# A one-core hybrid attention layer: first modulation sums shared with TensorE, an accumulator per token tile at the end, another machine model in the scheduler

## The chip, the cores and the metric

One core of a Trainium2 chip runs the whole layer in one launch. The metric is the device time in microseconds (us) of one execution; the median over several executions is quoted, and one further execution is recorded by the hardware profiler.

## What is computed

One decoder layer on 256 tokens of 2048 channels, in float32:

```
mod = silu(c) @ w_ada + b_ada                      # 2048 -> 3 x 2048: shift, scale, gate
h = rms_norm(x, g_pre) * (1 + scale) + shift
proj = h @ w_in                                    # 2048 -> 20032
a  = mla(q, kv_a) * silu(z_mla);    y_mla = a @ w_mla_proj      # 16 heads, causal, low-rank k and v
bb = dilated(qkv) * silu(z_dil);    y_dil = bb @ w_dil_proj     # 3 groups x 8 heads, softmax over all 3
merged = sigmoid(gl_mla) * y_mla + sigmoid(gl_dil) * y_dil
out = merged @ w_o
x = x + gate * rms_norm(out, g_post)
```

## The kernel before, in words

**Projections.** Tokens stand in two tiles t of 128. Every weight block goes through `load_split` (L227): a DMA on SP's queue brings 512 KB as `raw` (8 buffers), ScalarE (ACT) rounds it to the high part `whi` (L235), VectorE (DVE) subtracts to get the low part `wlo` (L236; 4 buffers each). `multiply` (L239) then makes three products on TensorE (PE), hi x hi, hi x lo and lo x hi, as matmuls of 128 tokens by 512 columns (L246). One projection group of 512 output columns is 8 such blocks, 96 matmuls, into one accumulator `acc`. In most of the kernel there are two accumulators; a group is copied out by ACT (L578 and others) before its accumulator serves the next group but one.

**Start.** `w_ada` is needed before the first h. Its shift and scale columns come in 7 pieces (`PIECES`, 3 blocks of 128 channels in the first). For a piece, DVE multiplies each of 16 row blocks with a column of silu(c) and adds it to `ada` (L172, L174); matmuls with ones (`pt_ada`, L187) add over the partitions; `adasc`, `colmul` and `colsh` are made from that (L189 to L192) and `make_h` (L203) builds the operand hTh, hTl. While piece 1 is summed, PE has nothing to do but `keep_busy` matmuls whose result is not used (L150). Later pieces are summed while PE works through the groups listed in `head` (`visit`, L526).

**Attention between projections.** `dil_attention(quad)` (L468) does four heads, twice. A head D: transposes of q and k and their copies (`qk_t`, L452), then for each t three score matmuls (s_D, L482), the masked maximum on DVE (L435), the exponential on ACT (L439), transposes of the probabilities (pt_pD, L448), a copy by ACT (L449), the product with v (pv_D, L491) and DVE's product with the gate (L493). After the quad, `transpose_split` (L417) turns the result for the projection. The MLA loop (L626) has f = 0 to 3, each with two pairs j of two heads M: scores s_M (L667 to L671), exponentials (L683), pt_pM, pv_M (L689 to L691), the gate product `av` (L694), and after four heads `transpose_split` to aT (L698); each f begins with the gate group `zm` whose SiLU (L629) empties its accumulator. In both, every step waits for the one before it.

**End.** `acc_o` groups of 512 or 256 columns; ACT squares each (L746), DVE multiplies it with the gate (L747). The last 256 columns are computed for t = 0, then t = 1, in one accumulator `acc_last` (L755); then the norm, and four adds of 512 columns with a DMA each (L766, L768).

**Order.** The program text gives dependencies. In which order an engine executes its instructions is chosen by the tile scheduler when the context at L789 closes, from its own model of how long everything takes. Each engine then runs its list strictly in that order.

Of the kernel before, what the change touches and what calls it, by code (L numbers as in the profile page):

```python
# [9 lines left out]
F32 = mybir.dt.float32  # L10
# [3 lines left out]
ALU = mybir.AluOpType  # L14

P = 128
S = 256
D = 2048
KC = D // P
# [17 lines left out]
W_BUFS = 4  # L37
H_BUFS = 3
QK_BUFS = 4
WARM = 6  # L40
U_BUFS = 27
SCRATCH = 1024
PIECES = (3, 2, 3, 2, 2, 2, 2)
# [30 lines left out]
def hybrid_block(ctx: ExitStack, tc: tile.TileContext, x, c, positions, w_ada, b_ada, g_pre, g_post,  # L74
                 w_in, g_kv, w_kv_b, w_mla_proj, w_dil_proj, w_o, table, out):
    nc = tc.nc
    V, A, T = nc.vector, nc.scalar, nc.tensor

    cp = ctx.enter_context(tc.tile_pool(name="cp", bufs=1))
# [5 lines left out]
    def slot(shape, name, dt=F32):  # L85
        return up.tile(shape, dt, tag="u", name=name)

    def acc_tile(name):
        return banks["pool"].tile([P, 2, 512], F32, tag="acc", bufs=banks["acc"], name=name)

    def tp_tile(shape, name):
        return banks["pool"].tile(shape, F32, tag="b", bufs=banks["b"], name=name)
# [5 lines left out]
    xr = x[0].rearrange("(t p) d -> p t d", p=P)  # L98
    crow = cp.tile([16, P], F32, tag="crow", name="crow")
    rows = cp.tile([52, P], F32, tag="rows", name="rows")  # L100
# [4 lines left out]
    ident = tid[:, 0:P]  # L105
# [3 lines left out]
    for q in range(4):  # L109
        t = slot([P, 2, 512], f"xn{q}")  # L110
# [6 lines left out]
    ones = cp.tile([P, P], F32, tag="ones", name="ones")  # L117
# [3 lines left out]
    ccol = cp.tile([P, 16], F32, tag="ccol", name="ccol")  # L121
    pt = tp_tile([P, 16], "pt_c")
# [24 lines left out]
    def keep_busy(v):  # L147

        idle = tp_tile([P, 512], "idle")
        T.matmul(idle[:, :v.shape[-1]], ident, v, start=True, stop=True)  # L150

    def ada_steps(pi):

        a, nk = starts[pi], PIECES[pi]
        n = nk * P
        kb = max(1, RAW // (2 * n))
        acc = slot([P, 2, n], f"ada{pi}")
        steps = []
        src = w_ada[0].rearrange("(k p) (j d) -> p k j d", p=P, d=D)
        flat = acc.rearrange("p j n -> p (j n)")  # L160
        pt = tp_tile([P, 2, nk], f"pt_ada{pi}")

        def one(k0, kn):
            raw = wp.tile([P, RAW], F32, tag="raw", bufs=RAW_BUFS, name=f"raw_a{pi}_{k0}")
            v = raw[:, :kn * 2 * n].rearrange("p (k j n) -> p k j n", j=2, n=n)
            for k in range(kn):
                nc.sync.dma_start(v[:, k], src[:, k0 + k, 0:2, a * P:a * P + n])
            for k in range(kn):
                kk = k0 + k
                w = raw[:, k * 2 * n:(k + 1) * 2 * n]  # L170
                if kk == 0:
                    V.tensor_scalar(flat, w, ccol[:, kk:kk + 1], None, op0=ALU.mult)  # L172
                else:
                    V.scalar_tensor_tensor(flat, w, ccol[:, kk:kk + 1], flat, op0=ALU.mult, op1=ALU.add)  # L174
                if pi == 0 and kk >= KC - WARM:
                    keep_busy(v[:, k, 0, :])

        for k0 in range(0, KC, kb):
            steps.append(lambda k0=k0: one(k0, min(kb, KC - k0)))

        def finish():
            sc = sp.tile([P, 4], F32, tag="adasc", name=f"adasc{pi}")
            parts = [(b, b + 1) for b in range(nk)] if pi == 0 else [(0, nk)]
            for lo, hi in parts:
                for b in range(lo, hi):
                    for j in range(2):
                        T.matmul(pt[:, j, b:b + 1], acc[:, j, b * P:(b + 1) * P], ones[:, 0:1],  # L187
                                 start=True, stop=True)
                V.tensor_add(sc[:, lo:hi], pt[:, 1, lo:hi], bsc[:, a + lo:a + hi])  # L189
                V.scalar_tensor_tensor(colmul[:, a + lo:a + hi], sc[:, lo:hi], 1.0, gpre[:, a + lo:a + hi],  # L190
                                       op0=ALU.add, op1=ALU.mult)
                V.tensor_add(colsh[:, a + lo:a + hi], pt[:, 0, lo:hi], bsh[:, a + lo:a + hi])  # L192
                make_h(a + lo, a + hi)
            if pi == 0:
                for _ in range(2):
                    keep_busy(acc[:, 0, :])

        return steps, finish

# [63 lines left out]

    win = w_in[0]


    ssx = cp.tile([P, 2, 4], F32, tag="ssx", name="ssx")
    xT = []
    for q in range(4):
        xT.append(slot([P, 4, S], f"xT{q}"))  # L270
        for hp in range(2):
            pt = tp_tile([P, 2, 2, P], f"pt_x{q}{hp}")
# [5 lines left out]
        for t in range(2):  # L278
            j = sp.tile([P, 768], F32, tag="sm", name=f"junk_x{q}{t}")
            if t == 0:  # L280
                A.activation(j[:, 0:512], xn[q][:, t, :], AF.Square, accum_out=ssx[:, t, q:q + 1])
            else:
                V.tensor_tensor_reduce(j[:, 0:512], xn[q][:, t, :], xn[q][:, t, :], 1.0, 0.0,
                                       op0=ALU.mult, op1=ALU.add, accum_out=ssx[:, t, q:q + 1])
# [9 lines left out]
    pt = tp_tile([P, S], "pt_r")  # L294
    T.matmul(pt, ones, rdiag.rearrange("p t n -> p (t n)"), start=True, stop=True)
    V.tensor_copy(rstdT, pt)

    cols = cp.tile([P, 52], F32, tag="cols", name="cols")
    pt = tp_tile([P, 52], "pt_cols")
    T.transpose(pt, rows, ident[0:52, 0:52])  # L300
    V.tensor_copy(cols, pt)
    bsh, bsc, gpre = cols[:, 0:16], cols[:, 16:32], cols[:, 32:48]
    gkv = cols[:, 48:52]


    gacc = [None, None]
    gg = [None, None]
# [235 lines left out]
    for pi in range(len(PIECES)):  # L543
# [4 lines left out]
        if last:  # L548
            head_ps.__exit__(None, None, None)
            banks.update(pool=ctx.enter_context(tc.tile_pool(name="ps", bufs=1, space=bass.MemoryType.PSUM)),  # L550
                         acc=2, b=4)
# [21 lines left out]
    for g in range(1, 3):  # L573
        for s in range(3):
            nm = f"d{s}{g}1"
            acc = group(hT, win, KC, dil_col(s, g, 1), 512, nm)
# [7 lines left out]
    for t in range(2):  # L584
        j = sp.tile([P, 768], F32, tag="sm", name=f"junk_kv{t}")
# [7 lines left out]
    for k in range(4):  # L593
        pt = tp_tile([P, 2, P], f"pt_ckv{k}")
# [8 lines left out]
    for t in range(2):  # L603
        v = kpe[:, t:t + 1, :]
        rope(kp[:, t:t + 1, 0:64], v, cosM[:, t, 0:1, :], sinM[:, t, 0:1, :], 64, f"kp{t}")
    V.tensor_copy(kp[:, :, 64:128], kp[:, :, 0:64])
    pt = tp_tile([P, 2, P], "pt_kp")
# [9 lines left out]
    for h in range(2):  # L617
        r, o = slice(h * 64, (h + 1) * 64), slice((1 - h) * 64, (2 - h) * 64)
# [7 lines left out]
    for f in range(4):  # L626
        acc = group(hT, win, KC, C_ZMLA + f * 512, 512, f"zm{f}")
# [3 lines left out]
        for pr in range(2):  # L631
            j = 2 * f + pr
            gate_some(KC // UK // 2)
            while mq_done < 384 * (j + 1):
                acc = group(hT, win, KC, mq_done, 512, f"mq{mq_done // 512}")
# [7 lines left out]
            acc = group(ckv, wkv, 4, j * 512, 512, f"kv{j}")  # L643
# [5 lines left out]
            pt = tp_tile([P, 2, P], f"pt_qp{j}")  # L649
# [5 lines left out]
            for h in range(2):  # L655
                r, o = slice(h * 64, (h + 1) * 64), slice((1 - h) * 64, (2 - h) * 64)
                A.copy(qst[r, h, :], flat[r])
                V.tensor_tensor(qst[o, h, :], flat[r], qst[r, h, :].bitcast(F32), ALU.subtract)
            for h in range(2):
# [4 lines left out]
                for t in (1, 0):  # L664
                    nk = (t + 1) * P
                    o = 0 if t else S
                    T.matmul(sc[:, o:o + nk], qk[:, 0, t * P:(t + 1) * P], qk[:, 1, 0:nk],  # L667
                             start=True, stop=False)
# [5 lines left out]
                for t in (1, 0):  # L674
                    nk = (t + 1) * P
                    o = 0 if t else S
                    V.tensor_tensor_reduce(sm[:, o:o + nk], sc[:, o:o + nk], mm[t], 1.0, -3e38,
                                           op0=ALU.add, op1=ALU.max, accum_out=st[:, t:t + 1])
                V.tensor_scalar(st[:, 2:4], st[:, 0:2], -SC_MLA, None, op0=ALU.mult)
                for t in (1, 0):  # L680
                    nk = (t + 1) * P
                    o = 0 if t else S
# [10 lines left out]
                for t in range(2):  # L693
                    V.scalar_tensor_tensor(av[:, t, hs], pv[:, t, :], st[:, 6 + t:7 + t], zm[:, t, hs],  # L694
                                           op0=ALU.mult, op1=ALU.mult)
# [7 lines left out]
    part = []  # L703
    for n in range(4):
        acc = group(hT, win, KC, C_GLD + n * 512, 512, f"gd{n}")
        sg = slot([P, 2, 512], f"sgd{n}")
        A.activation(sg, acc, AF.Sigmoid)
        acc = group(bbT, w_dil_proj[0], 8, n * 512, 512, f"yd{n}")
# [3 lines left out]
    for n in range(4):  # L712
        acc = group(hT, win, KC, C_GLM + n * 512, 512, f"gm{n}")
# [16 lines left out]


    ssq_o = cp.tile([P, 2, 5], F32, tag="sso", name="sso")
    xre = []
    for n in range(4):
        t = slot([P, 2, 512], f"xre{n}")
        nc.scalar.dma_start(t, xr[:, :, n * 512:(n + 1) * 512])
        xre.append(t)
    ov = [slot([P, 2, 512], f"ov{n}") for n in range(4)]
    outr = out[0].rearrange("(t p) d -> p t d", p=P)
    blocks = [(0, 512), (512, 512), (1024, 512), (1536, 256), (1792, 256)]  # L740

    def out_block(i, t, acc):
        c0, n = blocks[i]
        m, o = divmod(c0, 512)
        j = sp.tile([P, 768], F32, tag="sm", name=f"junk_o{i}{t}")
        A.activation(j[:, 0:n], acc[:, t, :n], AF.Square, accum_out=ssq_o[:, t, i:i + 1])  # L746
        V.tensor_mul(ov[m][:, t, o:o + n], acc[:, t, :n], gg[m // 2][:, m % 2, o:o + n])  # L747

    for i, (c0, n) in enumerate(blocks[:-1]):
        acc = acc_tile(f"acc_o{i}")  # L750
        run(acc, mT, w_o[0], 0, KC, c0, n, f"o{i}")
        for t in range(2):
            out_block(i, t, acc)
    c0, n = blocks[-1]
    acc = acc_tile("acc_last")  # L755
    tiles = [(k, kn) + load_split(w_o[0], k, kn, c0, n, f"last_{k}") for k, kn in chunks(0, KC, n)]
    for t in range(2):
        for k, kn, whi, wlo in tiles:
            multiply(acc, mT, whi, wlo, k, kn, n, k == 0, k + kn == KC, (t,))
        out_block(4, t, acc)  # L760
        sq = cp.tile([P, 1], F32, tag=f"sq{t}", name=f"sq{t}")
        V.reduce_sum(sq, ssq_o[:, t, :], axis=mybir.AxisListType.X)
        ro = cp.tile([P, 1], F32, tag=f"ro{t}", name=f"ro{t}")
        rsqrt_mean(ro, sq, D, f"ro{t}", 1)
        for m in range(4):
            V.scalar_tensor_tensor(xre[m][:, t, :], ov[m][:, t, :], ro, xre[m][:, t, :],  # L766
                                   op0=ALU.mult, op1=ALU.add)
            (nc.sync if m % 2 else nc.scalar).dma_start(outr[:, t, m * 512:(m + 1) * 512], xre[m][:, t, :])  # L768


_INS = ("x", "c", "positions", "w_ada", "b_ada", "g_pre", "g_post", "w_in", "g_kv", "w_kv_b",
# [21 lines left out]
```

## Time and profile before

| | us |
|---|---|
| median of 3 runs | 1297.11 (1294.25 to 1297.4) |
| the profiled execution, its own time | 1296.44 |
| its span in the trace | 1294.6 |

Around the span lie 1296.44 - 1294.6 = 1.8 us. The page gives each engine's busy time over the span, then 40 slices; PEclk is TensorE's granted clock in tenths of full speed. The chain of waits follows the last instruction back to what released it; the wait view adds up, by instruction and releaser, the time in which an engine had nothing to run.

### The profile page before, as it was taken

Reading aid. Unit: us, or ns where it says so; the run is one execution under the profiler, and the core shown is the slowest. Engines: PE = TensorE matmul, PEld = TensorE weight load, DVE = VectorE, ACT = ScalarE, POOL = GpSimd, SP = SyncE. Lnnn points to the kernel's source line nnn. Section 1 sums busy time; section 2 is a strip of 40 time slices with the busy share of each in tenths; the row PEclk is TensorE's granted clock in tenths of the full one; section 3 lists DMA queues with packets and bytes.
Section 4 is the critical chain, followed back from the end, with each engine's and each line's share of the span. In section 5 each row is a group of like instructions: output and inputs, shape, how many; then the busy total and the mean of one; then the engine's idle time right before and its main releaser. Section 6 shows DMA issues by size and latency. Waiting matters only on the chain.

```text
span 1294.6 us, 16408 instructions
## 1 busy us (share of the span) xinstructions
PE 1263.7 (98%) x6063; PEld 1046.1 (81%) x6063; DVE 828.1 (64%) x1210; ACT 600.4 (46%) x775; POOL 0.2 (0%) x4
## 2 busy tenths in 40 slices
PE   4999999999999999999999999999999999999996
PEld 3888888888888888888878888788888888888886
DVE  6878887996974445549666585675444444565545
ACT  2555334344365444455545555555444444434442
POOL 0000000000000000000000000000000000000000
PEclk8899999999999999999999999999999999999999
DMA  9899988986552566526667485674666665565741
GB/s 331 297 309 328 319 276 283 309 281 215 170 158 82 182 194 195 164 79 206 233 205 256 125 318 159 209 250 127 193 194 193 195 195 195 198 221 184 259 147 65
DMA packets 158971, 275.00 MB, mean 212 GB/s; under 512 B 9574, under 2 KB 46636, under 8 KB 158892
## 3 DMA queue, kind: packets, MB, share of 16 engines
q1 hardware_dynamic: 156564, 268.70, 64.1%
q10 hardware_dynamic: 2328, 5.27, 1.2%
q8 instruction: 47, 0.77, 0.2%
q14 instruction: 32, 0.26, 0.1%
HBM read 271.83 MB, written 2.10 MB: 212 GB/s over the span
## 4 chain that ended last, share of the span: by engine, by line
PE 95%; DVE 3%; DMA 1%; ACT 1%; issue 1%; SPq 0%; DVEq 0%; ACTq 0%
PE acc_d L246 30%; PE acc_mq L246 10%; PE acc_gd L246 7%; PE acc_ym L246 7%; PE acc_gm L246 7%; PE acc_zm L246 6%; PE acc_o L246 6%; PE acc_zd L246 3%; PE acc_yd L246 3%; PE acc_kv L246 3%; PE acc_kva L246 2%; PE pv_D L491 1%; PE s_D L482 1%; DVE ada L174 1%; PE acc_last L246 1%; PE s_M L667 1%
## 5 line engine op out<-in xcount | busy, mean ns | idle before, releaser
L235 ACT CAST whi_d<-raw_d 128x1024 fp32r<-128x1024 f32 (+1 forms) x156 | 152.8, 987 | 194.1 <-PE acc_d L246 146.3
L236 DVE TENSOR_TENSOR wlo_d<-raw_d,whi_d 128x1024 fp32r<-128x1024 f32 (+1 forms) x156 | 176.5, 1139 | 66.4 <-ACT whi_d L235 64.4
L246 PE MATMUL acc_d<-whi_d,hTl 128*128 128x512 f32 x576 | 160.1, 394 | 0.0
L246 PE MATMUL acc_d<-whi_d,hTh 128*128 128x512 f32 x576 | 158.6, 393 | 1.4 <-DVE d L537 1.4
L246 PE MATMUL acc_d<-wlo_d,hTh 128*128 128x512 f32 x576 | 157.1, 391 | 0.0
L246 PEld LDWEIGHTS acc_d<-whi_d,hTh 128*128 128x128 f32 x576 | 107.8, 189 | 23.8 <-issue 1.8
L246 PEld LDWEIGHTS acc_d<-whi_d,hTl 128*128 128x128 f32 x576 | 108.3, 189 | 22.8 <-DVE hTl L213 0.7
L246 PEld LDWEIGHTS acc_d<-wlo_d,hTh 128*128 128x128 f32 x576 | 108.3, 188 | 22.5
L174 DVE SCALAR_TENSOR_TENSOR ada<-raw_a,ccol,ada 128x512 f32<-128x512 f32 (+1 forms) x105 | 86.5, 824 | 10.9 <-DMA raw_a<-in_w_ada 9.5
L236 DVE TENSOR_TENSOR wlo_mq<-raw_mq,whi_mq 128x1024 fp32r<-128x1024 f32 x48 | 58.5, 1221 | 23.4 <-ACT whi_mq L235 19.4
L235 ACT CAST whi_mq<-raw_mq 128x1024 fp32r<-128x1024 f32 x48 | 50.3, 1051 | 47.1 <-PE acc_mq L246 20.6
L236 DVE TENSOR_TENSOR wlo_gm<-raw_gm,whi_gm 128x1024 fp32r<-128x1024 f32 x32 | 39.2, 1225 | 45.4 <-ACT whi_gm L235 45.4
L236 DVE TENSOR_TENSOR wlo_ym<-raw_ym,whi_ym 128x1024 fp32r<-128x1024 f32 x32 | 39.1, 1223 | 32.9 <-ACT whi_ym L235 32.9
L236 DVE TENSOR_TENSOR wlo_gd<-raw_gd,whi_gd 128x1024 fp32r<-128x1024 f32 x32 | 39.2, 1224 | 32.4 <-ACT whi_gd L235 30.5
L235 ACT CAST whi_ym<-raw_ym 128x1024 fp32r<-128x1024 f32 x32 | 33.8, 1055 | 51.0 <-PE acc_ym L246 37.7
L236 DVE TENSOR_TENSOR wlo_o<-raw_o,whi_o 128x1024 fp32r<-128x1024 f32 x28 | 34.2, 1224 | 35.4 <-ACT whi_o L235 35.4
L235 ACT CAST whi_gm<-raw_gm 128x1024 fp32r<-128x1024 f32 x32 | 33.8, 1055 | 49.6 <-PE acc_gm L246 43.9
L246 PE MATMUL acc_mq<-wlo_mq,hTh 128*128 128x512 f32 x192 | 53.0, 393 | 0.0
L246 PE MATMUL acc_mq<-whi_mq,hTl 128*128 128x512 f32 x192 | 52.9, 394 | 0.0
L235 ACT CAST whi_gd<-raw_gd 128x1024 fp32r<-128x1024 f32 x32 | 33.7, 1053 | 40.5 <-PE acc_gd L246 20.4
L236 DVE TENSOR_TENSOR wlo_zm<-raw_zm,whi_zm 128x1024 fp32r<-128x1024 f32 x32 | 39.1, 1223 | 20.8 <-ACT whi_zm L235 18.2
L246 PE MATMUL acc_mq<-whi_mq,hTh 128*128 128x512 f32 x192 | 52.0, 392 | 0.0
(274 smaller groups left out, 2346.8 us busy)
## 6 DMA issues: line engine op xcount, KB each, us to landing
raw_d<-in_w_in SPq DMA_DIRECT2D x132, 512.0 KB, 4.5
raw_mq<-in_w_in SPq DMA_DIRECT2D x48, 512.0 KB, 4.6
raw_a<-in_w_ada SPq DMA_DIRECT2D x80, 256.0 KB, 4.6
raw_zm<-in_w_in SPq DMA_DIRECT2D x32, 512.0 KB, 3.7
raw_g<-in_w_ada SPq DMA_DIRECT2D x32, 512.0 KB, 4.1
raw_gd<-in_w_in SPq DMA_DIRECT2D x32, 512.0 KB, 4.4
raw_gm<-in_w_in SPq DMA_DIRECT2D x32, 512.0 KB, 4.5
raw_ym<-in_w_mla_proj SPq DMA_DIRECT2D x32, 512.0 KB, 3.9
```

Of the source, the lines that this page charges most:

```text
L174: V.scalar_tensor_tensor(flat, w, ccol[:, kk:kk + 1], flat, op0=ALU.mult, op1=ALU.add)
L235: A.copy(whi[:, :m], raw[:, :m])
L236: V.tensor_tensor(wlo[:, :m], raw[:, :m], whi[:, :m].bitcast(F32), ALU.subtract)
L246: T.matmul(acc[:, t, :n], opd.get(part, k0 + k, t), wt[:, k * n:(k + 1) * n], start=start and ph == 0 and k == 0, stop=stop and ph == 2 an ...
L482: T.matmul(sc[:, i * nk:(i + 1) * nk], qk[g][:, 0, t * P:(t + 1) * P], qk[g][:, 1, 0:nk], start=True, stop=True)
L491: T.matmul(pv, pT[:, b, :], dil[2, g, quad][:, kt, hs], start=b == 0, stop=b == nb - 1)
L667: T.matmul(sc[:, o:o + nk], qk[:, 0, t * P:(t + 1) * P], qk[:, 1, 0:nk], start=True, stop=False)
```

## The change

It has three parts. (1) Of the first piece's 16 row blocks, seven (`ROW_K`) are summed by TensorE: two matmuls of one output row by 384 columns each, into an accumulator `row`; ACT copies the row, six small matmuls (`pt_row`) turn it into columns, two DVE additions put it into the bias columns `cols`, which are transposed earlier for that. The idle matmuls go from six blocks to two, and from two to one after each `pt_ada`. (2) At the end each token tile has its own `acc_last`, its own `xre` and `ov` tiles of 1024 columns, and three output transfers of 1024, 768 and 256 columns; the last gate product comes behind the norm. (3) The tile context is opened with `schedule_with_timeline_sim=True`, so the scheduler orders all instructions by another machine model.

```diff
--- before.py
+++ after.py
@@ -37,7 +37,7 @@
...
-WARM = 6
+ROW_K = (1, 3, 5, 7, 9, 11, 13)
...
@@ -159,6 +159,19 @@
...
+        row = acc_tile("row") if pi == 0 else None
+
+        def rows_done():
+
+            part = slot([P, 2, n], "rowp")[0:1]
+            A.copy(part, row[0:1, :, 0:n])
+            pr = tp_tile([P, 2, nk], "pt_row")
+            for j in range(2):
+                for b in range(nk):
+                    T.matmul(pr[:, j, b:b + 1], part[0:1, j, b * P:(b + 1) * P], ones[0:1, 0:1],
+                             start=True, stop=True)
+            V.tensor_add(bsh[:, a:a + nk], bsh[:, a:a + nk], pr[:, 0, :])
+            V.tensor_add(bsc[:, a:a + nk], bsc[:, a:a + nk], pr[:, 1, :])
 
         def one(k0, kn):
             raw = wp.tile([P, RAW], F32, tag="raw", bufs=RAW_BUFS, name=f"raw_a{pi}_{k0}")
@@ -168,11 +181,17 @@
             for k in range(kn):
                 kk = k0 + k
                 w = raw[:, k * 2 * n:(k + 1) * 2 * n]
-                if kk == 0:
+                if pi == 0 and kk in ROW_K:
+                    for j in range(2):
+                        T.matmul(row[0:1, j, 0:n], ccol[:, kk:kk + 1], v[:, k, j, :],
+                                 start=kk == ROW_K[0], stop=kk == ROW_K[-1])
+                    if kk == ROW_K[-1]:
+                        rows_done()
+                elif kk == 0:
                     V.tensor_scalar(flat, w, ccol[:, kk:kk + 1], None, op0=ALU.mult)
                 else:
                     V.scalar_tensor_tensor(flat, w, ccol[:, kk:kk + 1], flat, op0=ALU.mult, op1=ALU.add)
-                if pi == 0 and kk >= KC - WARM:
+                if pi == 0 and kk > ROW_K[-1]:
                     keep_busy(v[:, k, 0, :])
 
         for k0 in range(0, KC, kb):
@@ -192,8 +211,7 @@
                 V.tensor_add(colsh[:, a + lo:a + hi], pt[:, 0, lo:hi], bsh[:, a + lo:a + hi])
                 make_h(a + lo, a + hi)
             if pi == 0:
-                for _ in range(2):
-                    keep_busy(acc[:, 0, :])
+                keep_busy(acc[:, 0, :])
 
         return steps, finish
 
@@ -262,6 +280,13 @@
         return acc
 
     win = w_in[0]
+
+    cols = cp.tile([P, 52], F32, tag="cols", name="cols")
+    pt = tp_tile([P, 52], "pt_cols")
+    T.transpose(pt, rows, ident[0:52, 0:52])
+    V.tensor_copy(cols, pt)
+    bsh, bsc, gpre = cols[:, 0:16], cols[:, 16:32], cols[:, 32:48]
+    gkv = cols[:, 48:52]
 
 
     ssx = cp.tile([P, 2, 4], F32, tag="ssx", name="ssx")
@@ -294,13 +319,6 @@
     pt = tp_tile([P, S], "pt_r")
     T.matmul(pt, ones, rdiag.rearrange("p t n -> p (t n)"), start=True, stop=True)
     V.tensor_copy(rstdT, pt)
-
-    cols = cp.tile([P, 52], F32, tag="cols", name="cols")
-    pt = tp_tile([P, 52], "pt_cols")
-    T.transpose(pt, rows, ident[0:52, 0:52])
-    V.tensor_copy(cols, pt)
-    bsh, bsc, gpre = cols[:, 0:16], cols[:, 16:32], cols[:, 32:48]
-    gkv = cols[:, 48:52]
 
 
     gacc = [None, None]
@@ -730,42 +748,50 @@
 
 
     ssq_o = cp.tile([P, 2, 5], F32, tag="sso", name="sso")
-    xre = []
-    for n in range(4):
-        t = slot([P, 2, 512], f"xre{n}")
-        nc.scalar.dma_start(t, xr[:, :, n * 512:(n + 1) * 512])
-        xre.append(t)
-    ov = [slot([P, 2, 512], f"ov{n}") for n in range(4)]
-    outr = out[0].rearrange("(t p) d -> p t d", p=P)
+    xre, ov = [], []
+    for t in range(2):
+        for m in range(2):
+            xt = slot([P, 1024], f"xre{t}{m}")
+            nc.scalar.dma_start(xt, x[0, t * P:(t + 1) * P, m * 1024:(m + 1) * 1024])
+            xre.append(xt)
+            ov.append(slot([P, 1024], f"ov{t}{m}"))
     blocks = [(0, 512), (512, 512), (1024, 512), (1536, 256), (1792, 256)]
 
-    def out_block(i, t, acc):
-        c0, n = blocks[i]
-        m, o = divmod(c0, 512)
+    def square(i, t, acc):
+        n = blocks[i][1]
         j = sp.tile([P, 768], F32, tag="sm", name=f"junk_o{i}{t}")
         A.activation(j[:, 0:n], acc[:, t, :n], AF.Square, accum_out=ssq_o[:, t, i:i + 1])
-        V.tensor_mul(ov[m][:, t, o:o + n], acc[:, t, :n], gg[m // 2][:, m % 2, o:o + n])
+
+    def gated(i, t, acc):
+        c0, n = blocks[i]
+        m, o = divmod(c0, 1024)
+        g = gg[m].rearrange("p a n -> p (a n)")
+        V.tensor_mul(ov[2 * t + m][:, o:o + n], acc[:, t, :n], g[:, o:o + n])
 
     for i, (c0, n) in enumerate(blocks[:-1]):
         acc = acc_tile(f"acc_o{i}")
         run(acc, mT, w_o[0], 0, KC, c0, n, f"o{i}")
         for t in range(2):
-            out_block(i, t, acc)
+            square(i, t, acc)
+            gated(i, t, acc)
     c0, n = blocks[-1]
-    acc = acc_tile("acc_last")
     tiles = [(k, kn) + load_split(w_o[0], k, kn, c0, n, f"last_{k}") for k, kn in chunks(0, KC, n)]
     for t in range(2):
+        acc = acc_tile(f"acc_last{t}")
         for k, kn, whi, wlo in tiles:
             multiply(acc, mT, whi, wlo, k, kn, n, k == 0, k + kn == KC, (t,))
-        out_block(4, t, acc)
+        square(4, t, acc)
         sq = cp.tile([P, 1], F32, tag=f"sq{t}", name=f"sq{t}")
         V.reduce_sum(sq, ssq_o[:, t, :], axis=mybir.AxisListType.X)
         ro = cp.tile([P, 1], F32, tag=f"ro{t}", name=f"ro{t}")
         rsqrt_mean(ro, sq, D, f"ro{t}", 1)
-        for m in range(4):
-            V.scalar_tensor_tensor(xre[m][:, t, :], ov[m][:, t, :], ro, xre[m][:, t, :],
-                                   op0=ALU.mult, op1=ALU.add)
-            (nc.sync if m % 2 else nc.scalar).dma_start(outr[:, t, m * 512:(m + 1) * 512], xre[m][:, t, :])
+        for i, (a, e) in enumerate(((0, 1024), (1024, 1792), (1792, 2048))):
+            if e == 2048:
+                gated(4, t, acc)
+            m = 2 * t + a // 1024
+            v = xre[m][:, a % 1024:a % 1024 + e - a]
+            V.scalar_tensor_tensor(v, ov[m][:, a % 1024:a % 1024 + e - a], ro, v, op0=ALU.mult, op1=ALU.add)
+            (nc.sync if i % 2 else nc.scalar).dma_start(out[0, t * P:(t + 1) * P, a:e], v)
 
 
 _INS = ("x", "c", "positions", "w_ada", "b_ada", "g_pre", "g_post", "w_in", "g_kv", "w_kv_b",
@@ -786,7 +812,7 @@
...
-    with tile.TileContext(nc) as tc:
+    with tile.TileContext(nc, schedule_with_timeline_sim=True) as tc:
         hybrid_block(tc, *args)
     r = run_bass_kernel_spmd(nc, [arrays], core_ids=[0])
     return r.results[0]["out"]
```

**TensorE, third head of the first quad (D02), token tile 0 and what follows.** s_D are scores, pt_pD the transposed probabilities, pv_D the product with v, acc_d a projection group. Before:

```order
L482 MATMUL s_D_3290<-qkD_3274 128x128
L482 MATMUL s_D_3290<-qkD_3281 128x128
L246 MATMUL acc_d_3589<-whi_d_0_3592,hTl_284 128x512
L246 MATMUL acc_d_3589<-wlo_d_0_3593,hTh_283 128x512
L482 MATMUL s_D_3290<-qkD_3288 128x128
L246 MATMUL acc_d_3589<-wlo_d_0_3593,hTh_283 128x512 x3
L246 MATMUL acc_d_3589<-whi_d_2_3610,hTh_283 128x512 x4
L246 MATMUL acc_d_3589<-whi_d_2_3610,hTl_284 128x512
L448 MATMUL pt_pD_3301<-tid,sm_D_3294 128x128 x3
L246 MATMUL acc_d_3589<-whi_d_2_3610,hTl_284 128x512 x3
L491 MATMUL pv_D_3306<-d_205,pT_D_3300 128x128
```

The same head now:

```order
L500 MATMUL s_D_3299<-qkD_3283 128x128
L500 MATMUL s_D_3299<-qkD_3290 128x128
L500 MATMUL s_D_3299<-qkD_3297 128x128
L466 MATMUL pt_pD_3310<-tid,sm_D_3303 128x128 x3
L509 MATMUL pv_D_3315<-d_205,pT_D_3309 128x128
L509 MATMUL pv_D_3315<-d_206,pT_D_3309 128x128
L509 MATMUL pv_D_3315<-d_207,pT_D_3309 128x128
L500 MATMUL s_D_3320<-qkD_3283 128x256
L500 MATMUL s_D_3320<-qkD_3290 128x256
L500 MATMUL s_D_3323<-qkD_3297 128x256
L466 MATMUL pt_pD_3333<-tid,sm_D_3325 128x128 x3
L466 MATMUL pt_pD_3338<-tid,sm_D_3325 128x128 x3
```

The projection matmuls that stood between the steps of this head are gone from here; they stand in the quad's first two heads, 18 to 27 at a time. The fourth head reads the same way.

**ScalarE, end of the first quad (last head's copies, the casts of the transposed result, the copies that empty the accumulators).** Before:

```order
L449 COPY pT_D_3396<-pt_pD_3397 128x384
L449 COPY pT_D_3396<-pt_pD_3402 128x384
L414 CAST bbTh_3415<-pt_bb_3417 128x512
L414 CAST bbTh_3415<-pt_bb_3424 128x512
L235 CAST whi_d_0_3739<-raw_d_0_3737 128x1024
L235 CAST whi_d_2_3757<-raw_d_2_3755 128x1024
L235 CAST whi_d_4_3775<-raw_d_4_3773 128x1024
L235 CAST whi_d_6_3793<-raw_d_6_3791 128x1024
L578 COPY d_3734<-acc_d_3589 128x1024
```

Now:

```order
L467 COPY pT_D_3405<-pt_pD_3406 128x384
L467 COPY pT_D_3405<-pt_pD_3411 128x384
L432 CAST bbTh_3424<-pt_bb_3426 128x512
L596 COPY d_3743<-acc_d_3598 128x1024
L596 COPY d_3890<-acc_d_3745 128x1024
L253 CAST whi_d_8_3967<-raw_d_8_3965 128x1024
```

Two full accumulators (3598 and 3745) are now copied out behind the last head's steps; before, one unfinished group ran on across the end of the quad.

**VectorE, end of the first piece's sums.** Now:

```order
L193 SCALAR_TENSOR_TENSOR ada_215<-raw_a_15_283,ccol,ada_215 128x768
L173 TENSOR_TENSOR cols<-cols,pt_row 128x3
L174 TENSOR_TENSOR cols<-cols,pt_row 128x3
L254 TENSOR_TENSOR wlo_d_0_326<-raw_d_0_323,whi_d_0_325 128x1024
L254 TENSOR_TENSOR wlo_d_2_344<-raw_d_2_341,whi_d_2_343 128x512
L208 TENSOR_TENSOR adasc_288<-pt_ada_216,cols 128x1
```

Before, `adasc` stood right behind the last `ada`, and the first `wlo_d` ten rows further on. On SP's queue the 655 KB load of `msk`, which before came at 165 us, now stands between the loads of row blocks 7 and 8 of the first piece.

## Rows read from the trace of the kernel before

**Rows 1.** The page: busy time by engine; granted clock of TensorE in 40 slices.

```profile
PE 1263.7 (98%) x6063; PEld 1046.1 (81%) x6063; DVE 828.1 (64%) x1210; ACT 600.4 (46%) x775; POOL 0.2 (0%) x4
PEclk8899999999999999999999999999999999999999
```

**Rows 2.** Waits of PE: instruction, releaser: us in total, times, longest.

```profile
PE pt_ada L187 <- DVE ada L174: 2.7, 1, 2.7
PE pt_pM L448 <- ACT sm_M L683: 1.6, 2, 0.8
...
PE acc_d L246 <- DVE d L537: 1.4, 1, 1.4
PE acc_last L246 <- DVE ov L747: 1.1, 1, 1.1
```

**Rows 3.** Chain of waits, first quad and after: start us, us, what.

```profile
398.66 1.30 PE s_D L482 x6
...
411.59 1.30 PE s_D L482 x6
...
418.84 117.23 PE acc_d L246 x517
```

**Rows 4.** Timeline, one dilated head: start us, us, engine, line, op, out<-in.

```profile
385.57 1.46 PE L482 MATMUL s_D<-qkD 128*128 128x256 f32 x6
...
389.40 0.82 PE L448 MATMUL pt_pD<-tid,sm_D 128*128 128x128 f32 x6
...
390.52 1.60 PE L491 MATMUL pv_D<-d,pT_D 128*128 128x128 f32 x12
...
394.52 0.38 PE L482 MATMUL s_D<-qkD 128*128 128x128 f32 x2
...
396.59 0.51 PE L448 MATMUL pt_pD<-tid,sm_D 128*128 128x128 f32 x3
...
397.73 0.94 PE L491 MATMUL pv_D<-d,pT_D 128*128 128x128 f32 x6
```

**Rows 5.** Timeline, one MLA head.

```profile
785.05 0.61 DVE L694 SCALAR_TENSOR_TENSOR av<-pv_M,st_M,zm 128x128 f32<-128x128 f32 x2 [0.31 <-PE pv_M L691]
...
785.18 0.27 PE L457 MATMUL pt_qkM<-tid,kv 128*128 128x128 f32 x1
...
786.22 0.61 PE L667 MATMUL s_M<-qkM 128*128 128x256 f32 x2
...
787.18 0.27 PE L671 MATMUL s_M<-kpl,qst 128*128 128x128 f32 x1
...
789.19 0.56 PE L448 MATMUL pt_pM<-tid,sm_M 128*128 128x128 f32 x3
...
790.32 0.49 PE L689 MATMUL pv_M<-kv,pT_M 128*128 128x128 f32 x2
```

**Rows 6.** Timeline of ACT, end of the second quad.

```profile
590.23 1.08 ACT L414 CAST bbTh<-pt_bb 128x512 fp32r<-128x512 f32 x2 [1.75 <-PE pt_bb L424]
...
594.07 1.28 ACT L629 ACT_TABLE_LOAD   x1
595.36 1.03 ACT L629 ACTIVATE zm<-acc_zm 128x1024 f32<-128x1024 f32 x1
```

**Rows 7.** Windows: us, busy of PE, PEld, DVE, ACT, POOL, granted clock, DMA share, GB/s.

```profile
30.00:31.00 1.00, 0.00 (x0) 0.00 (x0) 1.00 (x1) 0.00 (x0) 0.00 (x0) 1.00 1.09 346
33.00:34.00 1.00, 1.00 (x3) 0.70 (x3) 0.83 (x4) 0.20 (x2) 0.00 (x0) 0.50 1.05 363
39.00:40.00 1.00, 1.00 (x6) 0.79 (x5) 0.95 (x3) 0.90 (x1) 0.00 (x0) 0.86 0.84 213
300.00:370.00 70.00, 68.59 (x331) 56.96 (x330) 59.90 (x115) 32.13 (x38) 0.00 (x0) 1.00 0.59 181
```

**Rows 8.** The start: a window (columns as in rows 7), and a group of DVE.

```profile
20.00:30.00 10.00, 6.83 (x15) 2.96 (x13) 9.68 (x13) 1.04 (x1) 0.00 (x0) 0.72 1.07 373
...
L236 DVE TENSOR_TENSOR wlo_d<-raw_d,whi_d 128x1024 fp32r<-128x1024 f32 (+1 forms) x156 | 176.5, 1139 | 66.4 <-ACT whi_d L235 64.4
```

**Rows 9.** Timeline of DVE at the end: the last adds.

```profile
1288.28 2.74 DVE L766 SCALAR_TENSOR_TENSOR xre<-ov,ro,xre 128x512 f32<-128x512 f32 x4
```

## The prediction

> **What bounds the kernel now.** I read the page first: PE is busy 1263.7 of 1294.6 us and holds its full clock in every slice but the first two [rows 1]. Then PE's waits: behind the start the largest three add up to 1.6 + 1.4 + 1.1 = 4.1 us [rows 2]. So PE's own list is the path, and there is nearly nothing left to win between the start and the end. An attention head is a chain through PE, DVE and ACT, and yet PE hardly waits there. The chain of waits shows why: a dilated head returns every 411.59 - 398.66 = 12.93 us [rows 3], and the order shows 24 projection matmuls in each, standing just where PE would wait for the softmax. One costs 117.23 / 517 = 0.227 us [rows 3], so 24 are 5.44 us, and a head's own matmuls 12.93 - 5.44 = 7.5 us. The reader is to see that those 24 cost nothing extra only because they have to be done anyway; a head without them waits.
>
> **What a bare head waits.** From the timeline [rows 4], between the end of one step and the start of the next that depends on it: for the 256-key tile, scores end at 385.57 + 1.46 = 387.03 and the transposes start at 389.40, 2.37 us; from their end, 390.22, to pv at 390.52, 0.30. For the 128-key tile 394.90 to 396.59 is 1.69, and 397.10 to 397.73 is 0.63. The two matmuls that stand before the third score pair cover a copy, 2 x 0.227 = 0.45. The sum is 5.44, the same as the 24 matmuls that fill it: nothing of the cover is spare. For an MLA head [rows 5]: the copy of q and k, 785.45 to 786.22, 0.77; softmax, 787.45 to 789.19, 1.74; the copy of the probabilities, 789.75 to 790.32, 0.57; together 3.1 us.
>
> **The scheduler's other model.** The work is the same, the order is not. In the new list the first heads of a quad carry 18 to 30 projection matmuls between two steps, until both accumulators are full; then there is nothing left to put in, and the last heads stand bare. I count from the order:
> - Dilated heads: third and fourth of each quad bare, 4 x 5.44 = 21.8. The second head of quad 0 bares one copy, 0.30; that of quad 1 bares its 256-key tile, 2.37 + 0.30 = 2.67. Sum 24.8.
> - MLA heads: the last of f = 1 and the last two of f = 3 bare, 3 x 3.1 = 9.3.
> - Ends of the four f and of the second quad. Both accumulators are full, and the one that the next group needs is emptied by ACT behind the cast of the transposed result, a table load and the SiLU or sigmoid. PE sees DVE's product 0.61 [rows 5], one cast 1.08 / 2 = 0.54, the load 1.28 and the activation 1.03 [rows 6], 3.5 in all; the four transposes of the second half run beside the cast, at 0.82 / 6 = 0.14 [rows 4] at most 0.55, so that 2.9 to 3.5 is left, and I take 3.3. Five times, 16.5. At the end of the first quad a plain copy stands there, 1.0 (about the activation of rows 6).
>
> That is 24.8 + 9.3 + 16.5 + 1.0 = 51.6. The waits that the old order had in the middle, 1.6 + 1.4 = 3.0 [rows 2], I take as gone: -3.0. Upper bound: the second pair of f = 3 also bares a chain over `qst`, which no row here separates. Lower bound: if only the softmax waits stay and half of each end, 4 x (2.37 + 1.69) + 2.37 + 3 x 1.74 + 5 x 1.65 = 32.1, less 3.0.
>
> **The clock.** Before, PE idled 2.7 us behind DVE's last `ada` [rows 2]. In that gap the granted clock still read 1.00, and then 0.50 at 33 us, though PE was busy again, until 0.86 in 39 to 40 [rows 7]. Some 6.4 us at half speed lose 3.2. The 1.4 us wait at 313 us left the clock at 1.00 over its whole window [rows 7]. The bared softmax waits of 2.37 lie between these two, the five ends (3.3, with 0.6 of it ahead of the transposes) at the longer one. Bounds: none falls, 0, or all five fall, 5 x 3.2 = 16. I take half, +8.
>
> The Trainium skill says more: TensorE: Matmul & The Clock Gate, section "A second HAM failure mode: psum-queue depth-cycling", describes a kernel whose PE paused often and briefly between groups of matmuls, and lost throughput to throttling and warming again between the bursts. By that rule the bare heads as a whole would run at an oscillating clock. This case's trace shows one gap that did this and one shorter that did not; the rule's time is that of my second rival, 1370 to 1394, whose working stands below without it.
>
> **The start.** DVE's part falls from 16 sums to 9, so that the 2.7 us [rows 2] by which it ends behind the loads may go: -2.7 at best. Against it: the load queue is saturated there, 373 GB/s [rows 8], and `msk`, 655 KB, is now put ahead of row block 8: 655 / 373 = 1.8 us later. Behind the last sum two splits now precede `adasc`, one whole and one half, 1.5 x 1.14 = 1.7 [rows 8]. The bias additions and `pt_row` add a few tenths. So -2.7 to +4; I take 0. The four idle blocks that are dropped stood where PE waited anyway; what they covered was the clock, and its bound is the 3.2 above, counted in the range.
>
> **The end.** The second tile's matmuls no longer wait for the first tile's product: -1.1 [rows 2]. The four adds of 2.74 [rows 9] become three of the same bytes, with one product moved between them; the first transfer now starts after a 1024-wide add, 0.7 later, the last is shorter. Bounds -2 and +1; I take -0.5.
>
> **Sum.** 51.6 - 3.0 + 8 + 0 - 0.5 = +56.1 on the profiled execution's own 1296.44 is 1352.5. The median is 0.67 above that execution, so 1353.2, rounded to 1353.
>
> **Rivals.**
> - Bare chains are cheaper than the gaps say: without casts and additions of projections between them DVE and ACT answer sooner. For it: DVE's and ACT's steps there stand in a row with splits. Against it: in rows 4 nothing stood between the scores and the exponential of the 128-key tile, and the wait was still 1.69. It gives the lower bound, 32.1 - 3.0 - 0.5 = +28.6, 1326.
> - The clock falls in the bare heads too. Their own PE work, 4 x 7.5 = 30 us, then takes up to twice the time, and six resumptions lose 3.2 each, 19: 1297.1 + 48.1 + 49 = 1394 at worst, 1370 if half of it. For it: the fall at 33 us [rows 7]. Against it: a bare head is 58% busy and its longest gap, 2.37, is shorter than the one that brought the fall.
> - Faster: the start decides. If the seven row blocks on PE take away the 2.7, the middle waits and the end give 3.0 + 2.0, and the bare waits are hidden, the time is 1297.1 - 7.7 = 1289. It decides only if the waits of all bare stretches together stay under 7.7 us, a seventh of the sum; since PE runs its list in order and nothing stands between the steps, I see no way but a chain seven times as fast.
> - The flag does less than the order shows, or the waits equal the gains: 1297.
>
> **How the numbers follow.** Forecast 0.63 (its own range 1334 to 1372), cheaper chains 0.14, clock in the heads 0.18, faster 0.03, no change 0.02. The range 1322 to 1388 takes in the first two and the lower half of the third. 0.3% is 3.9 us, about what a measurement of this kernel can tell from none: faster 0.03, same 0.02, slower 0.95.
>
> **What would show it.** In PE's waits: pt_pD behind sm_D with some 2.4 and 1.7 us a time, in third and fourth heads only; pt_pM in the bare MLA heads; acc_kv and acc_gd behind zm and sgd, some 3 us each, five in all. PE's busy sum stays near 1264 if the clock holds, and grows by what it loses. The granted clock falls, if anywhere, behind the ends. Wrong would be a PE wait sum under 20 us, or one whose largest item is the start. If PE's busy time grows by over 25 us, the second rival holds.

## The result and the profile after

The changed kernel takes 1359.94 us in the median (1357.36 to 1363.1), the kernel before 1297.26: ratio 1.0491, 95% interval 1.0471 to 1.0511. 1353 was forecast. The profiled execution took 1357.36 us, its span is 61.0 us longer than before. The page first, to be laid beside [rows 1]: busy time, granted clock, the chain by engine.

```profile
PE 1287.2 (95%) x6093; PEld 1065.9 (79%) x6093; DVE 819.5 (60%) x1203; ACT 600.7 (44%) x774; POOL 0.2 (0%) x4
PEclk9999999999999799998999999999799999999999
PE 89%; DMA 4%; ACT 3%; DVE 2%; issue 1%; SPq 0%; DVEq 0%; ACTq 0%
```

PE's share fell, but its busy time rose by 23.5 us with the work nearly unchanged, and the clock row has dips that were not there. So two things happened: PE waits 61.0 - 23.5 = 37.5 us longer, and it works more slowly for a while. PE's waits name the first (compare [rows 2]):

```profile
PE pt_pD L466 <- ACT sm_D L457: 17.5, 9, 2.3
PE acc_kv L264 <- ACT zm L647: 7.4, 4, 3.3
PE pt_pM L466 <- ACT sm_M L701: 4.8, 3, 1.6
PE row L186 <- DMA raw_a<-in_w_ada: 4.1, 4, 2.2
...
PE pv_D L509 <- ACT pT_D L467: 3.0, 6, 0.6
PE acc_zd L264 <- ACT whi_zd L253: 2.9, 2, 2.5
PE pt_av L442 <- DVE av L712: 2.4, 2, 1.2
PE pv_M L707 <- ACT pT_M L467: 2.3, 4, 0.6
...
PE acc_gd L264 <- ACT sgd L725: 2.2, 1, 2.2
PE s_M L685 <- ACT qkM L477: 2.0, 3, 0.7
PE acc_d L264 <- DVE d L555: 1.4, 1, 1.4
PE s_D L500 <- ACT qkD L477: 1.1, 4, 0.3
```

The dilated heads are 17.5 + 3.0 + 1.1 = 21.6, the MLA heads 4.8 + 2.3 + 2.0 = 9.1, the ends of the f loop and of the second quad 7.4 + 2.4 + 2.2 = 12.0. Each is a chain that now stands open. The rows of `row` and `acc_zd` lie in the start. PE's timeline of one bare dilated head:

```profile
443.92 1.46 PE L500 MATMUL s_D<-qkD 128*128 128x256 f32 x6
447.69 1.52 PE L466 MATMUL pt_pD<-tid,sm_D 128*128 128x128 f32 x6 [2.31 <-ACT sm_D L457]
449.19 1.65 PE L509 MATMUL pv_D<-d,pT_D 128*128 128x128 f32 x6
```

and the chain of waits at the end of f = 0:

```profile
737.82 0.45 PE pt_av L442 x4
...
738.30 0.59 ACT aTh L432
...
738.90 1.28 ACT L647
...
740.19 1.03 ACT zm L647
...
741.27 7.32 PE acc_kv L264 x24
```

The six transposes of the head shown took 0.82 us in [rows 4] and take 1.52 here. Windows of 1 us (columns as in [rows 7]) say why: the clock is still 1.00 while PE pauses (446 to 447 us), and at its lower level, 0.50, when PE works again.

```profile
446.00:447.00 1.00, 0.00 (x0) 0.00 (x0) 0.48 (x3) 0.40 (x1) 0.00 (x0) 1.00 0.00 0
448.00:449.00 1.00, 1.00 (x6) 0.81 (x4) 0.00 (x0) 0.34 (x1) 0.00 (x0) 0.50 0.00 0
450.00:451.00 1.00, 1.00 (x6) 1.00 (x6) 0.00 (x0) 0.00 (x0) 0.00 (x0) 0.50 0.00 0
...
464.00:465.00 1.00, 1.00 (x5) 1.00 (x6) 0.00 (x0) 0.42 (x1) 0.00 (x0) 0.50 0.00 0
473.00:556.00 83.00, 83.00 (x370) 68.75 (x369) 43.72 (x57) 35.79 (x36) 0.00 (x0) 1.00 0.67 191
```

From such windows over a whole span I add up two numbers for each run: PE's idle time, and an estimate of what the clock takes, busy time x (1 - granted clock). "Middle" is from 330 us to 20 us before the end. The kernel before was measured again beside each experiment, with medians of 1294.0 to 1296.2 us, and the ratios below are to those.

| run (profiled execution) | median us | middle: PE idle | middle: taken by the clock |
|---|---|---|---|
| before | 1297.26 | 2.7 | 0.0 |
| changed kernel | 1359.94 | 42.9 | 19.7 |
| e1 flag only | 1366.39 | 43.2 | 33.4 |
| e2 no flag | 1294.68 | 2.6 | 0.0 |
| e3 quads covered | 1338.23 | 30.5 | 11.8 |
| e4 all covered | 1322.98 | 21.1 | 1.7 |
| e9 casts too | 1315.67 | 13.5 | 4.9 |
| e5 old order, four bare heads | 1328.26 | 19.7 | 14.5 |
| e6 the same, idle matmuls | 1316.09 | 9.0 | 0.0 |
| e10 zm copied | 1356.55 | 37.7 | 26.1 |

Start and end are small beside that. The last chain step of the start, DVE's addition to d, begins at 318.13 us and began at 313.66: +4.5. From the last group's first matmul to the end of the span it is 1355.6 - 1334.63 = 21.0 us and was 1294.6 - 1272.41 = 22.2: -1.2. The traces of all runs agree on this: from the first `acc_last` record on, the four with the old end (before, e1, e5, e6) take 22.4 us, the ten with the new one 21.1 to 21.2.

### The profile page after: what moved, and what is told of

Same layout as the page of the kernel before. It is cut to its first block, busy times and chain, and to the rows that moved or that the text cites. A ratio compares the mean times of both kernels' runs of the same rounds, so it can differ in the third digit from the quotient of the medians.

```text
span 1355.6 us, 16403 instructions
## 1 busy us (share of the span) xinstructions
PE 1287.2 (95%) x6093; PEld 1065.9 (79%) x6093; DVE 819.5 (60%) x1203; ACT 600.7 (44%) x774; POOL 0.2 (0%) x4
## 4 chain that ended last, share of the span: by engine, by line
PE 89%; DMA 4%; ACT 3%; DVE 2%; issue 1%; SPq 0%; DVEq 0%; ACTq 0%
PE acc_d L264 27%; PE acc_mq L264 10%; PE acc_zm L264 6%; PE acc_gd L264 6%; PE acc_ym L264 6%; PE acc_gm L264 6%; PE acc_o L264 6%; PE acc_kv L264 4%; PE acc_yd L264 3%; PE acc_zd L264 3%; PE pv_D L509 2%; DMA raw_d<-in_w_in 1%; PE acc_kva L264 1%; DMA raw_a<-in_w_ada 1%; PE s_D L500 1%; PE s_M L685 1%
## 5 line engine op out<-in xcount | busy, mean ns | idle before, releaser
L264 PE MATMUL acc_d<-whi_d,hTl 128*128 128x512 f32 x576 | 156.8, 390 | 0.0
L193 DVE SCALAR_TENSOR_TENSOR ada<-raw_a,ccol,ada 128x512 f32<-128x512 f32 (+1 forms) x98 | 79.5, 811 | 15.2 <-DMA raw_a<-in_w_ada 14.4
```

The costliest lines, as they stand in the source:

```text
L264: T.matmul(acc[:, t, :n], opd.get(part, k0 + k, t), wt[:, k * n:(k + 1) * n], start=start and ph == 0 and k == 0, stop=stop and ph == 2 an ...
```

## The experiments

**Which part.** e1 is the kernel before with `schedule_with_timeline_sim=True` alone, e2 the changed kernel without it.

> The kernel before with the scheduler's other machine model and nothing else. Theory (the order with bare attention heads, and the clock falls behind them, make the time): its order shows the same bare heads as the changed kernel, so 1352 to 1364 us; PE waits of pt_pD behind sm_D again near 17 us in 9 waits. Rival (the row sums on PE at the start, or the end, are a good part of the 62 us): under 1340 us.

> The changed kernel with the scheduler's former machine model: row sums on PE and the accumulator per token tile alone. Theory (both parts together are worth what the prediction took, the wait of 1.1 us at the end and at most 2.7 us at the start): 1292 to 1298 us. Rival (the row sums bring their own waits at the start, as the 4.1 us of row behind raw_a in the changed kernel's trace): 1300 to 1304 us.

e1: ratio 1.0556 (1.0538 to 1.0575). e2: 0.9990 (0.9978 to 1.0002), no difference that can be told. So the flag makes the whole loss, and the edits by hand are worth nothing measurable. e1 came 2 us over its range and takes 6 us more than the changed kernel: its waits are the changed kernel's (43.2 and 42.9), its clock loses more.

**Giving the cover back.** e3 and e4 keep the flag and add order edges, which make an instruction stand behind another on its engine without waiting for it. Projection matmul number n after an attention block may not stand ahead of the step that it should cover:

```diff
+    def follow(ins):
+        hold = [a for thr, a in fill["after"] if thr <= fill["n"]]
+        if hold:
+            tc.add_manual_dep(ins.ins, hold[-1].ins.name,
+                              mybir.DependencyInfo(mybir.DependencyClass.NoSync, mybir.DependencyReason.DATA),
+                              reason="fill")
+        fill["n"] += 1
...
-                    T.matmul(acc[:, t, :n], ...)
+                    follow(T.matmul(acc[:, t, :n], ...))
...
+                fill["after"].append((ends[2 * t], last))
```

`ends` are sums of the counts that the old order had, 2, 8, 3, 10 and 1 in a dilated head (more in a quad's first); e3 does it in the quads, e4 in the MLA loop too. e9 adds edges on ACT: a weight cast whose buffer comes free only after the scores stands behind the exponential.

> The changed kernel with the order edges of e4 in the two dilated quads only; the MLA loop keeps the other model's order with its bare heads and ends. It divides e4's 37 us. Theory by the prediction's terms (dilated heads 24.8 of 51.6, and most of the clock's falls, which the changed kernel's trace shows in the quads): two thirds come back here, 1332 to 1340 us. Rival (the MLA loop with its five ends is the larger part): over 1345 us.

> The changed kernel, other machine model kept, but with order edges (no waits) that hold projection matmuls back, so that 24 stand in each dilated head and 43 in each pair of MLA heads, about as in the kernel before. Theory (missing cover is the cause): the attention waits fall from some 37 us to under 8, the clock stays at full speed behind the start, 1298 to 1308 us (the start's 4 us remain). Rival (the other model's order costs elsewhere, in loads, casts or accumulators): over 1325 us.

> The kernel of e4 (cover restored), with order edges on ScalarE as well: a weight cast whose buffer comes free only after the scores stands behind the exponential, not ahead of it. Theory (e4's remaining 21 us of waits between the start and the end are casts and splits that the other model puts ahead of a softmax step): pt_pD behind sm_D goes from 7.4 to under 2 us, time 1310 to 1316 us. Rival (the remainder comes from loads or accumulators): 1321 us or more.

e3: 1.0341 (1.0314 to 1.0369), 1338 us, in its range. e4: 1.0216 (1.0202 to 1.0231), 1323 us, between both expectations: cover brings back 37 of 63 us, 22 of them in the quads, and nearly all that the clock took (19.7 to 1.7). But PE still waits 21.1 us in the middle, so the waits did not fall as far as expected. Two rows of e4's PE waits, and its ACT around one softmax:

```profile
PE pt_pD L477 <- ACT sm_D L468: 7.4, 9, 1.2
PE s_M L709 <- ACT qkM L488: 7.0, 6, 1.2
```

```profile
406.19 1.05 ACT L253 CAST whi_d<-raw_d 128x1024 fp32r<-128x1024 f32 x1 [1.28 <-PE acc_d L275]
407.14 0.61 ACT L468 ACTIVATE sm_D<-sm_D,st_D 128x384 f32<-128x384 f32 x1
```

The exponential could have started at 406.2, when DVE's last step before it ended; the cast, itself late because PE had just freed its buffer, holds it up 0.9 us. In e9 the same two, in the other order:

```profile
403.91 0.62 ACT L473 ACTIVATE sm_D<-sm_D,st_D 128x384 f32<-128x384 f32 x1 [1.43 <-DVE st_D L472]
...
404.52 1.03 ACT L253 CAST whi_d<-raw_d 128x1024 fp32r<-128x1024 f32 x1
```

pt_pD behind sm_D is gone from PE's waits, and e9 takes 1.0152 (1.0136 to 1.0168), 1316 us. So the other model's order costs in at least two places, on PE and on ACT. The 19 us that e9 still has over the kernel before are 13.5 - 2.7 = 10.8 of waits and 4.9 of clock in the middle, and 4 at the start. Its largest waits in the middle stand behind copies within the MLA heads (s_M behind qkM 4.0, pv_M behind pT_M 3.6); what in the order makes them was not tested.

**Taking the cover away in the old order.** e5 is the kernel before, no flag, with one edge for each quad: no following projection matmul stands ahead of the fourth head's last pv, except those that heads one and two had.

```diff
+        fill["after"].append((55 if quad else 103, last))
```

e6 adds idle matmuls in the two softmax waits of those heads.

> The kernel before, former machine model, with order edges that let no projection matmul stand in the third and fourth head of each quad: four bare heads, nothing else. Theory: 4 x 5.4 = 22 us of waits, and falls of the clock as in the changed kernel, some 2 us for each of the four heads: 1320 to 1330 us. Rival (the chains are cheap, or the scheduler's model matters in another way): under 1312 us.

> The four bare heads of e5, with idle matmuls (2 for the 128-key tile, 3 for the 256-key tile) between the scores and the transposes, where PE otherwise waits; their result is not used. Theory (14.5 of e5's extra 33 us are TensorE at half clock, because PE paused): the clock stays at full speed, the waits are filled but not shortened, and 12 to 15 us come back: 1312 to 1317 us, and up to 3 more because the idle matmuls run a little over the waits. Rival (PE's extra busy time has another cause): 1327 us or more.

e5: 1.0255 (1.0238 to 1.0271), +33 us: 19.7 - 2.7 = 17.0 of waits and 14.5 of clock. Its time lay in the range by errors that cancel: 22 of waits and some 8 of clock were expected. e6: 1.0159 (1.0145 to 1.0174), 1316 us, as forecast. The softmax wait of PE in e5 and in e6:

```profile
PE pt_pD L459 <- ACT sm_D L450: 14.9, 8, 2.3
```

```profile
PE pt_pD L459 <- ACT sm_D L450: 2.8, 8, 0.4
```

Clock rows of the page, e5:

```profile
PEclk8999999999998999987999999999999999999999
```

and e6:

```profile
PEclk8999999999999999999999999999999999999999
```

From the scores' end to the transposes it is as long in e6 as in e5 (1.65 us for the 128-key tile, 2.3 for the 256-key tile at full clock); PE only does useless work in it, and 12 us come back. That separates the two costs of a bare chain: waiting, and the clock after it. They are of like size here.

**One end.** e10 empties the accumulator by a copy, and the SiLU works on the copy.

```diff
-        A.activation(zm, acc, AF.Silu)
+        A.copy(zm, acc)
+        A.activation(zm, zm, AF.Silu)
```

> The changed kernel, but the zm accumulator is emptied by a plain copy, and the SiLU with its table load works on the copy afterwards; TensorE's order is the same, instruction by instruction. Theory (at the ends PE waits for the accumulator, and the table load of 1.28 us stands in that wait): acc_kv behind zm goes from 7.4 to 3 us or less, 4 us or a little more come back, 1352 to 1356 us. Rival (the next group waits for something else there, or the clock makes the difference): 1359 us or more.

```profile
PE acc_kv L264 <- ACT zm L647: 2.5, 2, 1.8
```

The wait fell from 7.4 to 2.5 us, as expected; the time by 3.4, to 1356.55, half a microsecond over its range (ratio 1.0477, 1.0455 to 1.0499, which overlaps with the changed kernel's), as its clock took more in the profiled run. The wait is shown to be the accumulator's, the gain in time is not.

**The start and the end alone.** e7 is the change's end alone; e8 adds three idle matmuls where PE waited 2.7 us for the last sums.

```diff
                 if pi == 0 and kk >= KC - WARM:
-                    keep_busy(v[:, k, 0, :])
+                    for _ in range(4 if kk == KC - 1 else 1):
+                        keep_busy(v[:, k, 0, :])
```

> The kernel before with the change's end alone (two accumulators, tiles of 1024 columns, three transfers). Theory (the end is worth 1.2 us, as from the first matmul of the last group to the end of the span in the changed kernel's trace, and the row sums cost about as much at the start): 1293 to 1295 us, ratio 0.998 to 0.9995. Rival (row sums help and the end does not): 1296 us or more, above the kernel with both.

> The kernel of e7, with three more idle matmuls on the last row block of the first piece, in the 2.7 us in which PE waits for the last sums. Theory (the clock fell at 33 us because of that gap, and costs 3 us until 39 us): clock 1.00 from 31 us on, 1290 to 1292 us. Rival (the first groups wait for their operands anyway, so that a faster clock there only waits): as e7.

e7: 1.0000 (0.9989 to 1.0010), 1295.9 us, above its range; the 1.2 us that the traces show at the end are too little to be told in the time. e8: 0.9993 (0.9984 to 1.0003), 1294.7 us beside 1296.2, and not the 1292 or less expected. The clock did what was expected, but PE then waited for the operands:

```profile
33.00:34.00 1.00, 0.68 (x7) 0.58 (x5) 0.45 (x3) 0.00 (x0) 0.00 (x0) 1.00 1.06 367
34.00:35.00 1.00, 0.67 (x5) 0.59 (x6) 0.76 (x5) 0.51 (x1) 0.00 (x0) 1.00 1.09 352
```

The clock's fall at 31 to 33 us does not come every time either: e6, with the start of the kernel before, stayed at 1.00 from 28 us on without such matmuls. No version here is faster than the kernel before by more than the measurement can tell.

**Why the start is later.** e11 issues `msk` where it was (`tc.keep_in_program_order`), e12 also puts the two early splits behind the first h. Only the start is read.

> The changed kernel with the 655 KB load of msk issued where it was before, some 200 rows later on SP's queue. Only the start is read: the sums of the third piece's pt_ada begin at 112.9 us in the kernel before and at 117.1 in the changed one. Theory (the load stands in a saturated queue ahead of the first piece's second half): 1.8 us earlier, about 115.3 us. Rival (the first groups' loads wait for buffers that DVE frees late, whatever stands ahead): 116.5 us or later.

> As e11, and the two splits of the first weight blocks on DVE stand behind the first adasc, colsh, colmul and h, not ahead of them. Theory (they hold up the first h by their 1.9 us): pt_ada of the first piece's second block and the first acc_d come 1.5 to 2 us earlier than in e11, and the third piece's pt_ada begins at 113 to 114 us. Rival (the splits are needed by then anyway, and PE waits for them instead): as e11.

The third piece's sums on PE, in the changed kernel, e11 and e12:

```profile
117.08 1.39 PE L206 MATMUL pt_ada<-ones,ada 128*128 128x1 f32 x12
```

```profile
114.78 1.39 PE L206 MATMUL pt_ada<-ones,ada 128*128 128x1 f32 x12
```

```profile
114.88 1.39 PE L206 MATMUL pt_ada<-ones,ada 128*128 128x1 f32 x12
```

How far single executions can be read here is shown by runs whose PE lists are the same up to this point. With the old start (before, e5, e6, e7) these sums begin at 111.1 to 114.5 us, with the changed one (changed kernel, e3, e4, e9, e10) at 116.2 to 118.3. The clock differs between executions of one list: from 33 to 41 us it reads 1.00 in e6 and 0.50 in e7. So a loss of some 4 us is clear of the spread. e11 and e12 lie below the whole second group, by 1.3 to 3.5 us, but the clock has a part in that. Ahead of its fall the load's price can be read alone: `pt_row` begins at 29.2 and 29.3 us in the changed kernel and e10, at 27.8 in e11 and at 28.2 in e12, all four at 1.00 until then, so it is 1.1 to 1.5 us. e12 does not settle the splits: its clock read 0.50 from 31 to 33 us, where that of e11 stayed at 1.00.

The flag alone (e1, 111.31) and the row sums alone (e2, 114.08) lie inside the first group, so neither is shown to shift the start by itself, although e1 issues `msk` as early as the changed kernel does (11.9 and 11.7 us). Only together they make 4. A piece of that stands in the waits above: `acc_zd` behind `whi_zd`, 2.5 us at 94.92, for a cast that waits for its load. All seven runs with both parts have this wait, with 1.6 to 3.2 us, the others for 0.2 at most. Why it takes both stays open.

The totals of e11, 1357.62, and e12, 1361.64, single runs, are no lower than the changed kernel's profiled 1357.36; in the middle their clock took 22.3 and 24.7 us where the changed kernel's took 19.7.

## Why the prediction was right, and where it was not

The likeliest case came true, and the time lies 7 us over the forecast. Its steps:

- **The bare heads.** Dilated heads were put at 24.8 and show 21.6; MLA heads at 9.3 and show 9.1. The softmax pauses are the ones read off the covered trace: 2.31 for 2.37, 1.6 for 1.74. That the gap between scores and transposes in the covered order is the wait in the bare one held to 0.15 us. The small pauses behind copies came out shorter or were filled, so a bare dilated head of e5 waits 17.0 / 4 = 4.3 us and not 5.44. e4 shows that cover is what was missing, e5 that its loss does it in the old model's order too.
- **The ends.** Put at 16.5 + 1.0, they show 12.0, and the end of the first quad shows no wait. ACT's chain from the cast to the end of the SiLU or sigmoid takes 2.9 us at all four ends of f, as the prediction had it, but PE does not wait for all of it: transposes run beside the chain, and DVE's product, forecast at 0.61, does not stand ahead of it. At f = 0 PE pauses 1.22 + 0.99 = 2.2 us, and 2.2 at each of the other three. Only the end of the second quad costs 3.3 (the idle time before each row is in brackets):

```profile
648.65 1.69 PE L264 MATMUL acc_kv<-whi_kv,ckvh 128*128 128x512 f32 x4 [3.31 <-ACT zm L647]
...
739.70 0.59 PE L442 MATMUL pt_av<-tid,av 128*128 128x128 f32 x2 [1.22 <-DVE av L712]
...
741.27 2.07 PE L264 MATMUL acc_kv<-whi_kv,ckvh 128*128 128x512 f32 x4 [0.99 <-ACT zm L647]
```

- **The clock.** This is the term that was mis-sized: +8, with 0 to 16 as bounds, for falls behind the five ends only, at 3.2 us each. It took 19.7 us in the middle. A single fall in the middle took half of what was put for it, 1.5 to 1.7 us, but most falls came in the bare heads, which the second rival had said: 14.0 us at 447 to 452, 457 to 469, 625 to 629, 638 to 643 and 963 to 977 us. Behind two of the ends it was 3.3 (649 to 653, 741 to 745), and 2.3 at 812 to 820, where the fall begins in the bare head ahead of the end. The argument against that rival, that a pause of 2.37 is shorter than the 2.7 that brought a fall, failed: a pause of 2.31 at 447.69 brought one, and one of 1.57 at 962.87 too. PE's busy time grew by 23.5 us, just under the 25 set as that rival's sign. What speaks for the rule of the Trainium skill named there (TensorE: Matmul & The Clock Gate, "A second HAM failure mode: psum-queue depth-cycling") is e6: pauses filled, no fall. The rival's price, 49 us, was too high.
- **The start.** Put at 0 with +4 as the upper bound; it was +4.5. The 1.8 us for `msk` was about right (1.1 to 1.5 at `pt_row`). The 1.7 us for the splits was too much: in e11 they hold up `adasc` by 0.6 us (`pt_ada` ends at 31.1, `adasc` starts at 31.7), in the changed kernel by nothing, as `pt_ada` itself came later.
- **The end.** -0.5 was forecast, -1.2 measured.

By size: waits 8 us too high (51.6 - 3.0 = 48.6 against 42.9 - 2.7 = 40.2), clock 12 too low, start 4.5 too low. That the sum came so near is in part luck, since the errors in the waits and in the clock cancel. The terms as measured add up to 40.2 + 19.7 + 4.5 - 1.2 = 63.2, and the profiled executions differ by 60.9; the clock's share, an estimate, may be a little large, as in e6, where 14.5 by this estimate gave back 12.2.

The rival of cheaper chains is refuted by the waits, the faster one by e2 (all that its parts can give is under 3 us). What the run does not show is the other model itself. The order it chose fits a model in which the steps of an attention chain take far longer than they do: in the first two heads of a quad it puts 18 to 33 projection matmuls between two steps, and in the first MLA head 22 matmuls, 5 us, where the covered order has 6 and the copy waited for takes 0.48. That is argued from the order.

## What to carry to other kernels

Where an engine that bounds the kernel also runs dependent chains, the filler between their steps is a stock: count how much each chain needs from the gaps in a covered trace, and look in the list of instructions whether the last chains still have some. A bare chain cost twice here, by its wait and by TensorE's clock after it; with nothing useful to put in, idle matmuls gave back the second part. And a scheduler's option is to be judged by its order alone first: here one flag cost 5%, while the edits beside it were worth nothing that can be measured.

## What was not expected of the hardware

Nearly the same waits lost quite different amounts to the clock: 19.7 us in the changed kernel's profiled execution and 33.4 in e1's, with PE's idle time equal within 0.3 us. That is not one odd execution: the mean granted clock is 0.972 to 0.977 in the changed kernel's four runs and 0.960 to 0.964 in those of e1. e10 is a closer pair. It has the changed kernel's PE list, and its edit acts only from the first `zm` on; from 330 us to there (646 us, in e10 653) PE idles 22.4 and 21.5 us, and the clock takes 9.2 and 17.7.

Nor does a pause's length decide alone. In the changed kernel a pause of 2.25 us at 612.19 left the clock at 1.00, and one of 2.25 at 638.67 was followed by a fall. The two pauses of 1.22 and 0.99 us around the transposes ahead of 741 us were followed by a fall (741 to 745 us), the same two ahead of 909 us were not. In the start, 3.25 us at 96.79 in e9 brought no fall, and 3.18 us at 96.10 in e10 did. In the middle a single fall took 1.5 to 1.7 us, a series in neighbouring heads up to 5.5. What decides between them wasn't settled.
